# A planner's clock that counts each TensorE product at another length

## The chip, the cores and the metric

One Trainium2 chip, one core. The metric is the device time of one execution in microseconds (us), as the median of several runs.

## The reference

One inference step of a two-layer hybrid decoder, for 512 prompt tokens and 8 x 8 sample tokens (576 columns together). Cut to its core:

```python
for l in range(DEPTH):                      # 2 layers, D_MODEL 1024, D_FF 2816
    h = rmsnorm(x, norm_mix[l])
    proj = h @ w_in[l]                      # q, k, v, z, gates, pool and short-conv inputs
    o_a = delta_mixer(...)                  # conv, l2norm, chunked gated delta rule, 4 heads
    o_b = pool_mixer(...)                   # means over windows of 2, 4, 8, 16
    o_c = sc_b * causal_dwconv(sc_c * sc_x, ...)
    x = x + concat([o_a, o_b, o_c]) @ w_out[l]
    h = rmsnorm(x, norm_ffn[l])
    gate = causal_dwconv(h @ w_ffn_gate[l], ...)
    x = x + (silu(gate) * (h @ w_ffn_up[l])) @ w_ffn_down[l]
y = rmsnorm(x, final_norm)
```

## The kernel before

Tokens lie along the free axis: 576 columns in two halves of 288 (`HALVES`). Each f32 operand of a large product is split into a high and a low part of 32-bit "fp32r" type, and one weight tile times one half is three TensorE matmuls of 128x128 by 128x288 (`mm3`, lines 494 to 500). A weight piece holds four 128x128 tiles. It is loaded into `wraw`, its high part `whi` is copied by ScalarE (ACT) and its low part `wlo` is subtracted by VectorE (DVE) (`_split`, lines 145 to 153). One output tile `m` takes two pieces, 48 matmuls. Where the text counts products, it means these matmuls.

Each engine runs its instructions in the order in which the Python program writes them. That order is made by a planner at build time. `_Trunk.clock` holds one clock for each engine; `spend` (line 279) moves one of them by an operation's estimated cost. DVE, ACT and GpSimd (POOL) operations cost a fixed part and a part by the element (lines 207 and 208: 0.068 + n/960 us, 0.093 + n/1200 us and 0.1 + n/300 us, and 0.07 us more for a scale operand); a hand-over from one engine to another costs `hop`, 0.18 us. A TensorE product is counted in `mm` (line 457). "Now" is the planner's TensorE clock.

Small work (the triangular solves `tri`, `delta`, `sample`, the norms, the convolution tails) is written as generators, called streams. After each three products, `tick` (line 345) lets streams take a step if the end of their last step, plus a wait by name (`WAIT`), is not later than now. A stream of priority 1 is held back while the planner's DVE or ACT clock is more than 2.5 us ahead of now (`busy`, line 350). `room(2)` (line 390) at the start of each output tile forces stream steps, earliest first, until at most two PSUM banks wait to be read. `pump` (line 184) writes out the split of weight pieces up to two ahead of the piece that is in use.

The stretch that the prediction speaks of is the start of the feed-forward part in each layer. Its gate and up products are written in tiles m = 0, 1, 2, ... (even: gate of hidden group j = m/2; odd: up). Tiles 0 to 5 read the input before it is normalised, `fh` and `fl`, and scale their results; tile 6 is the first to read the normalised `nh` and `nl`. `normed` (lines 1785 to 1793) makes these in eight streams of an ACT copy, a POOL product, an ACT copy and a DVE subtraction, added when tile 2 starts (line 1999). `evac_gu` copies a gate tile into `gpad` with three DVE operations; `gate_tail` (line 1838) then makes two POOL copies, an ACT product and two DVE steps (`gcv`), an ACT tanh, and for j < 3 a DVE step (`gcv<-gth,gcv`) and two DVE products (`gth`); `up_tail` (line 1877) follows with two DVE products (`gp`), which empty the banks that `room` counts, and then splits the result (`hh`, `hl`).

Of the kernel before, what the change touches and what calls it, by code (L numbers as in the profile page):

```python
# [8 lines left out]
F32 = mybir.dt.float32  # L9
F32R = mybir.dt.float32r  # L10
F16 = mybir.dt.float16
# [229 lines left out]
class _Trunk:  # L241
# [209 lines left out]
    def mm(self, out, lhsT, rhs, start=True, stop=True):  # L451
        n = 1
        for d in rhs.shape[1:]:
            n *= d
        m = lhsT.shape[-1]
        f = lhsT.dtype
        self.spend("tensor", max(n * (4 if f == F32 else 1) / 2400.0, m / (4800.0 if f == F16 else 600.0 if f == F32 else 1200.0)) + 0.0025)
        self.nc.raw.tensor.matmul(out, lhsT, rhs, start=start, stop=stop)  # L458

    def rsqrt(self, v, n, name, eng):  # L460
# [1686 lines left out]
```

## Time and profile before

| | us |
|---|---|
| median of 3 runs (1520.3 to 1522.63) | 1522.19 |
| the profiled execution's own time | 1521.63 |
| its span, first to last instruction | 1519.9 |
| TensorE busy in the span | 1481.7 |
| DVE, ACT, POOL busy in the span | 1061.9, 681.5, 344.8 |

The span is the profiled execution's time without 1.7 us around it. "Busy" of TensorE (PE) counts overlapped matmuls, whose ends are modelled; so spacings of products are taken from starts or from rows that merge many. PEclk is the granted TensorE clock as a share of full speed: 1.00 is 2.4 GHz and 0.5 is 1.2 GHz.

### The profile page before, as it was taken

What the parts mean: (1) busy time and instruction counts of PE and PEld (TensorE: products, weight loads), DVE (VectorE), ACT (ScalarE), POOL (GpSimd) and SP (SyncE); (2) the same over time, 40 slices, a digit from 0 to 9 for tenths busy, and PEclk for the clock granted to TensorE, in tenths of its full rate; (3) what the DMA queues carried; (4) which work ended last, traced back from release to release, by engine and by line L of the source; (5) the groups of instructions that cost most, each with busy time, mean ns of one, the idle gap of its engine ahead of it and who ended that gap; (6) DMA issues with size and microseconds to landing.
All of it is one profiled execution on the core that took longest, in us unless ns stands there. A gap on an engine that the chain in (4) does not pass through costs nothing.

```text
span 1519.9 us, 29654 instructions
## 1 busy us (share of the span) xinstructions
PE 1481.7 (97%) x11438; PEld 1434.4 (94%) x11438; DVE 1061.9 (70%) x2253; ACT 681.5 (45%) x1453; POOL 344.8 (23%) x754
## 2 busy tenths in 40 slices
PE   9999999999899999999999999999989999999997
PEld 7999898899899999999999988989989999999997
DVE  7887776667973686377667987766588647854865
ACT  6445665545441344134533546754445324432442
POOL 2211022305511231122011111232083013301310
PEclk9999999999999999999999999999999999999998
DMA  5111122332223132222422112025212322232222
GB/s 199 61 56 43 47 74 85 129 99 70 84 83 99 63 105 84 84 97 73 142 76 67 57 45 91 22 85 171 77 57 91 97 71 97 77 93 96 77 82 84
DMA packets 67278, 128.78 MB, mean 85 GB/s; under 512 B 7952, under 2 KB 13248, under 8 KB 67136
## 3 DMA queue, kind: packets, MB, share of 16 engines
q1 hardware_dynamic: 59808, 105.15, 22.0%
q0 software_dynamic: 6208, 20.56, 3.8%
q8 instruction: 89, 1.46, 0.4%
q10 hardware_dynamic: 1120, 1.18, 0.2%
q14 instruction: 53, 0.43, 0.1%
HBM read 116.36 MB, written 10.49 MB: 83 GB/s over the span
## 4 chain that ended last, share of the span: by engine, by line
PE 86%; DVE 6%; issue 5%; ACT 1%; POOL 1%; DMA 1%; SPq 0%; POOLq 0%; DVEq 0%; ACTq 0%
PE ps L458 73%; PE q L458 12%; PE ps L229 2%; DVE wlo L229 1%; DVE gcv L229 1%; DVE m L229 1%; DMA xr<-in_x_dram 1%; DVE nl L229 1%; ACT m L229 1%; DVE cv L229 0%; DVE sqacc L229 0%; POOL kr_t L229 0%; DVE gth L229 0%; DVE xl L229 0%; DVE gpad L229 0%
## 5 line engine op out<-in xcount | busy, mean ns | idle before, releaser
L229 DVE TENSOR_TENSOR wlo<-wraw,whi 128x512 fp32r<-128x512 f32 (+1 forms) x432 | 315.9, 746 | 81.6 <-ACT whi L229 80.3
L229 ACT ACTIVATE whi<-wraw 128x512 fp32r<-128x512 f32 (+1 forms) x432 | 257.3, 613 | 158.7 <-PE ps L458 148.4
L458 PE MATMUL ps<-xh,whi 128*128 128x288 f32 x768 | 244.4, 318 | 0.1
L458 PE MATMUL ps<-xl,whi 128*128 128x288 f32 x768 | 228.9, 298 | 0.3 <-DVE xl L229 0.3
L458 PE MATMUL ps<-xh,wlo 128*128 128x288 f32 x768 | 228.2, 297 | 0.4 <-DVE wlo L229 0.4
L458 PE MATMUL ps<-nh,wlo 128*128 128x288 f32 x704 | 209.6, 298 | 13.3 <-DVE wlo L229 13.3
L458 PE MATMUL ps<-nh,whi 128*128 128x288 f32 x704 | 210.3, 299 | 0.0
L458 PE MATMUL ps<-nl,whi 128*128 128x288 f32 x704 | 209.7, 298 | 0.0
L458 PE MATMUL ps<-hh,whi 128*128 128x288 f32 x704 | 208.5, 296 | 0.0
L458 PE MATMUL ps<-hl,whi 128*128 128x288 f32 x704 | 207.6, 295 | 0.0
L458 PE MATMUL ps<-hh,wlo 128*128 128x288 f32 x704 | 207.0, 294 | 0.0
L458 PEld LDWEIGHTS ps<-xh,whi 128*128 128x128 f32 x768 | 146.1, 190 | 10.5 <-issue 7.9
L458 PEld LDWEIGHTS ps<-nh,wlo 128*128 128x128 f32 x704 | 134.7, 191 | 13.8 <-DVE wlo L229 13.8
L458 PEld LDWEIGHTS ps<-xh,wlo 128*128 128x128 f32 x768 | 146.4, 191 | 0.9 <-DVE wlo L229 0.9
L458 PEld LDWEIGHTS ps<-xl,whi 128*128 128x128 f32 x768 | 146.5, 191 | 0.8 <-DVE xl L229 0.7
L229 DVE SCALAR_TENSOR_TENSOR xr<-ps,xr 128x288 f32<-128x288 f32 x96 | 41.4, 457 | 140.4 <-PE ps L458 139.9
L458 PEld LDWEIGHTS ps<-nl,whi 128*128 128x128 f32 x704 | 134.1, 191 | 0.0
L458 PEld LDWEIGHTS ps<-nh,whi 128*128 128x128 f32 x704 | 134.1, 190 | 0.0
L458 PEld LDWEIGHTS ps<-hh,wlo 128*128 128x128 f32 x704 | 132.6, 188 | 0.0
L458 PEld LDWEIGHTS ps<-hl,whi 128*128 128x128 f32 x704 | 132.1, 188 | 0.0
L458 PEld LDWEIGHTS ps<-hh,whi 128*128 128x128 f32 x704 | 131.9, 187 | 0.0
L229 POOL TENSOR_TENSOR wraw<-wraw,wraw 128x512 f32<-128x512 f32 x48 | 74.9, 1559 | 109.1 <-DVE wlo L229 84.5
(313 smaller groups left out, 3335.3 us busy)
## 6 DMA issues: line engine op xcount, KB each, us to landing
wraw<-in_w_gu_dram SPq DMA_DIRECT2D x176, 256.0 KB, 2.9
wraw<-in_w_in_dram SPq DMA_DIRECT2D x96, 256.0 KB, 2.7
wraw<-in_w_dn_dram SPq DMA_DIRECT2D x80, 256.0 KB, 2.7
wraw<-in_w_out_dram SPq DMA_DIRECT2D x32, 256.0 KB, 2.8
xr<-in_x_dram POOLq DMA_DIRECT2D x12, 288.0 KB, 5.6
vs<-in_st_delta_dram POOLq DMA_DIRECT2D x6, 512.0 KB, 4.7
out_s_delta_dram<-vs POOLq DMA_DIRECT2D x6, 512.0 KB, 3.3
spill<-xr POOLq DMA_DIRECT2D x8, 288.0 KB, 2.4
```

What stands on the lines that cost most here:

```text
L229: return f(*args, **kw)
L458: self.nc.raw.tensor.matmul(out, lhsT, rhs, start=start, stop=stop)
```

## The change

`mm` counts a product differently; the instructions that it issues are the same. For the type of the large products the count was max(n/2400, m/1200) + 0.0025 us, with n columns and m weight columns; it becomes max(0.00044 n + 0.0025, 0.111 m/128) + 0.004. For f32 it was max(4n/2400, m/600) + 0.0025 and becomes max(0.00175 n + 0.0025, 0.224 m/128); for f16 it was max(n/2400, m/4800) + 0.0025 and becomes max(0.00042 n + 0.0025, 0.028 m/128).

```diff
         m = lhsT.shape[-1]
         f = lhsT.dtype
-        self.spend("tensor", max(n * (4 if f == F32 else 1) / 2400.0, m / (4800.0 if f == F16 else 600.0 if f == F32 else 1200.0)) + 0.0025)
+        per, least = {F32: (0.00175, 0.224), F16: (0.00042, 0.028)}.get(f, (0.00044, 0.111))
+        self.spend("tensor", max(n * per + 0.0025, least * m / 128.0) + (0.004 if f not in (F32, F16) else 0.0))
         self.nc.raw.tensor.matmul(out, lhsT, rhs, start=start, stop=stop)
```

## Rows read from the trace of the kernel before

**Rows 1.** The page: its span.

```profile
span 1519.9 us, 29654 instructions
```

**Rows 2.** Waits of PE, whole run: us in total, times, longest us.

```profile
PE ps L458 <- DVE wlo L229: 13.7, 4, 6.7
PE ps L458 <- DVE m L229: 3.3, 9, 0.5
PE ps L458 <- ACT m L229: 2.7, 2, 1.7
```

**Rows 3.** Windows of 40 us: length, busy us (instructions) by engine, PEclk, DMA share, GB/s.

```profile
160.00:200.00 40.00, 37.14 (x344) 34.07 (x344) 28.74 (x64) 24.80 (x64) 5.91 (x17) 0.96 0.25 84
...
400.00:440.00 40.00, 40.00 (x303) 40.00 (x302) 31.06 (x50) 19.52 (x38) 9.53 (x17) 1.00 0.31 94
```

**Rows 4.** Chain of work, feed-forward part: start us, us, what, count.

```profile
427.43 11.12 PE q L458 x84
438.56 64.00 PE ps L458 x480
```

**Rows 5.** Timeline of PE, mixer of layer 0: start us, us, instruction, count.

```profile
121.11 0.62 PE L458 MATMUL ps<-m 128*128 128x128 f16 x8
121.60 0.61 PE L458 MATMUL ps<-m,m 128*128 128x128 f16 x8
```

**Rows 6.** Timeline of PE where tile 6 starts: idle before it, and releaser, in brackets.

```profile
379.69 0.29 PE L458 MATMUL ps<-nl,whi 128*128 128x288 f32 x1
386.63 0.61 PE L458 MATMUL ps<-nh,wlo 128*128 128x288 f32 x1 [6.65 <-DVE wlo L229]
```

**Rows 7.** Windows around it, same columns as rows 3.

```profile
346.00:360.00 14.00, 14.00 (x108) 14.00 (x107) 3.20 (x8) 10.88 (x19) 6.92 (x7) 1.00 0.25 77
360.00:379.60 19.60, 19.60 (x149) 19.60 (x149) 19.34 (x25) 7.97 (x12) 13.87 (x15) 1.00 0.17 55
379.60:386.60 7.00, 0.38 (x3) 0.15 (x2) 6.93 (x10) 1.33 (x3) 6.69 (x7) 0.90 0.00 0
386.60:393.40 6.80, 6.77 (x32) 6.77 (x33) 6.73 (x8) 3.09 (x6) 6.41 (x7) 0.60 0.26 77
393.40:401.70 8.30, 8.30 (x65) 8.30 (x64) 8.30 (x13) 5.52 (x13) 3.69 (x8) 1.00 0.35 115
```

**Rows 8.** Timeline of ACT: the ACT product of gate group 0.

```profile
355.10 0.78 ACT L229 ACTIVATE gcv<-gpad,prm 128x592 f32<-128x592 f32 x1
```

**Rows 9.** Timeline of DVE in the same stretch.

```profile
356.42 0.84 DVE L229 TENSOR_TENSOR wlo<-wraw,whi 128x512 fp32r<-128x512 f32 x1 [2.67 <-ACT whi L229]
360.15 0.92 DVE L229 TENSOR_TENSOR gpad<-ps,rn 128x288 f32<-128x288 f32 x3 [2.89 <-PE ps L458]
360.99 4.59 DVE L229 TENSOR_TENSOR wlo<-wraw,whi 128x512 fp32r<-128x512 f32 x3
365.50 2.87 DVE L229 SCALAR_TENSOR_TENSOR gcv<-gpad,prm,gcv 128x592 f32<-128x592 f32 x2
...
375.05 1.69 DVE L229 SCALAR_TENSOR_TENSOR gcv<-gpad,prm,gcv 128x592 f32<-128x592 f32 x2
376.65 1.38 DVE L229 SCALAR_TENSOR_TENSOR gcv<-gth,gcv 128x592 f32<-128x592 f32 x1
378.07 1.94 DVE L229 TENSOR_TENSOR gth<-gcv,rn 128x512 f32<-128x512 f32 x2
379.93 2.10 DVE L229 SCALAR_TENSOR_TENSOR gcv<-gpad,prm,gcv 128x592 f32<-128x592 f32 x2
381.95 1.36 DVE L229 SCALAR_TENSOR_TENSOR gcv<-gth,gcv 128x592 f32<-128x592 f32 x1
383.35 1.89 DVE L229 TENSOR_TENSOR gth<-gcv,rn 128x512 f32<-128x512 f32 x2
385.16 0.81 DVE L229 TENSOR_TENSOR gp<-ps,gth 128x288 f32<-128x288 f32 x2
385.89 1.89 DVE L229 TENSOR_TENSOR wlo<-wraw,whi 128x512 fp32r<-128x512 f32 x2
```

## The prediction

> **What bounds the kernel now.** I read the page first, for the span [rows 1], then the waits of PE, the windows of 40 us, and the timelines of the one stretch that the waits point to. In the feed-forward part PE never pauses: its windows are full, at full clock [rows 3], and the chain there is products alone [rows 4]. No reordering can shorten that. What can move is what PE loses elsewhere, and one wait stands out: four waits on `wlo` make 13.7 us, the longest 6.7 [rows 2]. It comes where tile 6 starts, 6.65 us of idle [rows 6]. Layer 1 has its twin, since 13.7 is twice 6.65 and little more. The clock falls behind it: over the next 6.8 us PE is granted 0.60 and starts 32 products [rows 7], where at full clock it would start 6.8 / 0.1333 = 51. That is 6.8 - 32 x 0.1333 = 2.5 us more. So each layer loses 6.65 + 2.5 = 9.15 us there. DVE makes PE wait: from 360.0 to 386.6 it is busy 19.34 + 6.93 = 26.3 of 26.6 us, while in the 14 us before it is busy 3.2 [rows 7]. The second place is the mixer, with short waits on the `tri` chains' tiles (`m`): 3.3 us on DVE and 2.7 us on ACT over both layers [rows 2], and granted clocks of 0.96 in such a window [rows 3].
>
> **What the change counts.** For 288 columns the old line gives 288/2400 + 0.0025 = 0.1225 us, the new one 0.00044 x 288 + 0.0025 + 0.004 = 0.1332. The chain shows 11.12/84 = 0.1324 and 64.00/480 = 0.1333 [rows 4]. So now moves 8.7% more for each product, and is right. f16 products of 128 columns stay at 0.056 (0.0558 and 0.0563); eight of them take 0.49 us to the next eight [rows 5], 0.061 each. f32 products of 128 columns go from 0.216 to 0.227. The large products carry the effect. No instruction is added, removed or changed in cost, so the direct cost is nothing; what changes is the order on each queue.
>
> The Trainium skill has a rule that speaks against this: TensorE: Matmul & The Clock Gate, section "Wait — 56ns, not 53.3ns?", states N/2.4 GHz plus about 2.5 ns between starts at full clock, which at 288 columns is 122.5 ns, the old line exactly. By it the new line would count too long. The trace does not agree, with 132 to 133 ns here.
>
> **The start of the feed-forward part, step by step.** I follow the planner's clocks by its own lines. The eight `normed` streams start when tile 2 starts. Their ACT copies cost 0.093 + 576/1200 + 0.07 = 0.643 us each, 5.14 together, and the ACT product of gate group 0 behind them 0.656; with a hop of 0.18 it ends 5.98 us after tile 2 began. Tile 2 has 48 products: 5.88 us by the old count, 6.39 by the new one. So now the two DVE steps `gcv` of group 0 just miss the end of tile 2, by 0.10 us; after the change they make it, by 0.41 us. At the end of tile 2 stands the copy of gate tile 2, whose planned start lies behind eight POOL products of 0.1 + 576/300 = 2.02 us. It throws the planner's DVE clock some 12 us ahead, and with that every priority-1 stream is held back until the planner's wait for the next weights.
>
> The trace shows the result. ACT has finished group 0's product at 355.9 [rows 8], DVE idles 2.89 us up to 360.15, and the two steps run at 365.50, behind the copy and three `wlo`, for 2.87 us [rows 9]. In the new order they stand ahead of the copy and fill that idle time: 2.87 us less (1.69 where the same two steps run quicker) in the run of DVE that PE waits for.
>
> The second effect is at the start of tile 5, where `room(2)` forces group 0's two `gp`. Now group 0 is so late that the steps of groups 1 and 2 come earlier in the forced order: 2.10 us of `gcv`, 1.36 and 1.89 us of a later step and `gth` [rows 9] go ahead of the `wlo` that tile 6 needs. With group 0 finished before, only its `gp` is forced; these 2.10 + 1.36 + 1.89 = 5.35 us go behind that `wlo`. Together it is ready 2.87 + 5.35 = 8.2 us sooner: 386.6 - 8.2 = 378.4, or about 379.5 if some of the moved work runs at its slower durations, against PE's arrival at 379.7. The wait of 6.65 us goes, and with it the 2.5 us of clock.
>
> What is late next: the 5.35 us now stand before the `wlo` of tile 7's first piece, with one `wlo`, two `gp` and a split of `hh`, about 1 + 0.8 + 1.4 more. DVE is done with that at some 379.7 + 9 = 388.7; PE wants it 48 products after 379.7, at 386.1. A wait of 2.6 us, perhaps one of about 1 us for tile 8, and a shorter fall of the clock, some 1 us. So each layer gains 9.15 - 2.6 - 1 - 1 = 4.5; I take 5, since the later waits overlap. Bounds: 1.4 us, if only the time that DVE idles is won and in its quick form (1.69 less some 0.3 of the wait for the ACT part), and 9.15 if no new wait comes. Two layers: 10 us, between 3 and 18.
>
> **The mixer.** Steps of the small chains are written sooner in products: a step of 1.5 us is followed after 11.3 products, not 12.2. Forced bursts get shorter, since more was done before them, and cover of 0.13 us for each step is lost. Most steps have no wait on PE [rows 2], so I take zero here, with -3 to +6 us: the gain is at most about half of the 6.0 us of waits on `m`, the loss as much again as these waits.
>
> **The sum.** The profiled execution: 1521.63 - 10 = 1511.6. The median of the runs lies 0.56 above it: 1512.
>
> **The rivals.**
>
> Only half of it: the stall moves on to tiles 7 to 9, since DVE's work is the same and it is busy through 401.7 [rows 7]. For: DVE has no idle time there. Against: it idled just before, and full windows follow with DVE at 31 of 40 [rows 3]. Each layer gains 1.4: 1519.4. Chance 0.12.
>
> All of it: DVE's work behind tile 6 is spread thinly enough. 1522.2 - 18.3 = 1504. Chance 0.13.
>
> It does not do what it says here: another gate (the 2.5 us rule, a lack of pads) keeps group 0 behind the copy. The margin of 0.41 us is small, but the chain of ACT copies is anchored at tile 2's start in either count. 1522. Chance 0.08.
>
> Slower: the old count's missing 8.7% was cover, since the planner's DVE and ACT costs are short too: it counts a `wlo` at 0.60 us, and the trace has 0.84 and 1.53 [rows 9]. With the true product length, chains of `tri` reach PE before their data. If the waits on `m` double, 6.0 us more, with the boundary unchanged: 1528. It decides when a quarter or more of the small steps now arrive less than 0.2 us after their data. Against: only 11 waits are on `m`. Chance 0.17. If the skill's rule above held here, this cover would not exist at all and this case would be the likeliest.
>
> **How the numbers follow.** My forecast, the two gcv moved and most of the stall gone, has 0.50: 1512, by its own bounds 1504 to 1519. 1502 to 1524 takes in all but the slower case. A measurement of this kernel tells about 0.2%, 3 us, from no change. Faster: 0.50 + 0.13 + half of 0.12 = 0.69; within: 0.06 + 0.08 = 0.14; slower 0.17.
>
> **What would show it.** The timeline of DVE after `gcv<-gpad` x2 ahead of the `gpad` copy near 360, and fewer `gcv` and `gth` between it and the `wlo` that tile 6 waits for; PE's waits on `wlo` under 4 us a layer; a granted clock above 0.60 in the 6.8 us after tile 6 starts; full feed-forward windows as before; waits on `m` about 6 us. I am wrong if `gcv` still stands behind the copy, if the wait reappears whole at tile 7, or if waits on `m` grow past 10 us.

## The result, and the profile after

The changed kernel takes 1556.2 us (median of 4 runs, 1554.0 to 1557.3) against 1521.2 for the kernel before on the same chip: ratio 1.0227, 95% interval 1.0211 to 1.0243. It is 35 us slower; the prediction said 9 to 10 faster. The profiled execution took 1553.98 us, with a span of 1552.2. `mm` has one line more, so line 458 of before is L459 here.

The page of the kernel after: its span, and TensorE's busy time.

```profile
span 1552.2 us, 29696 instructions
PE 1498.4 (97%) x11438; PEld 1443.6 (93%) x11438; DVE 1077.2 (69%) x2253; ACT 681.3 (44%) x1453; POOL 366.2 (24%) x754
```

The waits of PE in it, to be laid beside [rows 2]: total us, times, longest.

```profile
PE ps L459 <- DVE m L229: 16.1, 15, 2.9
PE ps L229 <- ACT ms L229: 7.3, 2, 3.7
PE ps L459 <- DVE wlo L229: 6.7, 9, 1.5
```

The wait on `wlo` that the prediction was about is down from 13.7 to 6.7 us, and its longest from 6.7 to 1.5. But the waits on `m` have grown from 3.3 to 16.1 us, and one on `ms` (a tile of the `sample` chain) has appeared, twice 3.7 us.

Where the time went is seen best by product number: the start of the n-th large product in the two traces, and the difference. After is behind by 1.5 us at product 144, 3.0 at 864, 20.7 at 1152 (the end of layer 0's input projection) and 19.9 at 1824, where tile 6 of the feed-forward part starts. There it gains 9.3 us in its first 30 products, and gives back 5.1 by product 2400: 15.7 behind. Layer 1 repeats it: 18.4 behind at its product 864, 37.4 at 1152, 32.6 at the end. So the feed-forward start gains 4.2 us a layer and each mixer loses about 20, of which 17.7 and 19.0 us lie in the last six tiles of the input projection. The windows of that stretch, the same columns as [rows 3], after:

```profile
200.00:240.00 40.00, 36.65 (x313) 33.13 (x312) 27.41 (x72) 25.48 (x86) 7.32 (x35) 0.96 0.06 18
240.00:280.00 40.00, 35.47 (x237) 30.35 (x235) 20.56 (x59) 17.80 (x59) 9.90 (x43) 0.87 0.21 73
280.00:320.00 40.00, 38.08 (x230) 32.88 (x229) 22.48 (x51) 17.77 (x41) 13.07 (x42) 0.91 0.43 151
```

and before:

```profile
200.00:240.00 40.00, 40.00 (x361) 36.73 (x361) 29.71 (x72) 28.25 (x88) 8.05 (x39) 1.00 0.08 24
240.00:280.00 40.00, 39.74 (x263) 33.10 (x263) 25.02 (x77) 21.68 (x75) 15.44 (x61) 0.96 0.23 81
280.00:320.00 40.00, 38.85 (x277) 36.89 (x277) 25.24 (x55) 18.55 (x40) 7.49 (x20) 1.00 0.53 176
```

PE was busy in 97% or more of each of these windows; now it is in 89 to 95%, and DVE and ACT do less in each window, not more: they are not overloaded. The clock goes with the waits (0.87 and 0.91 of full speed: stretches at 0.5, the 1.2 GHz level, that follow PE's idle times). In layer 0, from the first large product to product 1152, PE's idle time goes from 5.6 to 17.6 us, and half of the time at half clock, which is about what it costs while PE is busy, from 5.1 to 11.9. Together that is 18.8 of the 20.7 us.

### The profile page after: what moved, and what is told of

It is laid out like the page before. It is cut to its first block, busy times and chain, and to the rows that moved or that the text cites. A ratio compares the mean times of both kernels' runs of the same rounds, so it can differ in the third digit from the quotient of the medians.

```text
span 1552.2 us, 29696 instructions
## 1 busy us (share of the span) xinstructions
PE 1498.4 (97%) x11438; PEld 1443.6 (93%) x11438; DVE 1077.2 (69%) x2253; ACT 681.3 (44%) x1453; POOL 366.2 (24%) x754
## 3 DMA queue, kind: packets, MB, share of 16 engines
q1 hardware_dynamic: 59808, 105.15, 21.8%
## 4 chain that ended last, share of the span: by engine, by line
PE 75%; DVE 10%; issue 6%; POOL 4%; ACT 4%; DMA 1%; SPq 0%; POOLq 0%; DVEq 0%; ACTq 0%
PE ps L459 62%; PE q L459 11%; DVE m L229 2%; PE ps L229 2%; DVE wlo L229 2%; ACT m L229 2%; POOL hl L229 1%; POOL hh L229 1%; DMA xr<-in_x_dram 1%; DVE gcv L229 1%; DVE nl L229 1%; DVE cv L229 1%; ACT whi L229 0%; ACT vs L229 0%; DVE fl L229 0%
## 5 line engine op out<-in xcount | busy, mean ns | idle before, releaser
L229 DVE TENSOR_TENSOR wlo<-wraw,whi 128x512 fp32r<-128x512 f32 (+1 forms) x432 | 314.2, 742 | 77.8 <-ACT whi L229 76.7
L229 ACT ACTIVATE whi<-wraw 128x512 fp32r<-128x512 f32 (+1 forms) x432 | 257.8, 614 | 163.5 <-PE ps L459 146.3
L459 PE MATMUL ps<-xh,whi 128*128 128x288 f32 x768 | 248.0, 323 | 1.9 <-ACT m L229 1.4
L459 PE MATMUL ps<-xl,whi 128*128 128x288 f32 x768 | 230.6, 300 | 0.6 <-DVE xl L229 0.6
L459 PE MATMUL ps<-xh,wlo 128*128 128x288 f32 x768 | 230.0, 299 | 0.2 <-DVE wlo L229 0.2
L459 PE MATMUL ps<-nh,wlo 128*128 128x288 f32 x704 | 208.2, 296 | 6.5 <-DVE wlo L229 6.5
L459 PE MATMUL ps<-nh,whi 128*128 128x288 f32 x704 | 208.3, 296 | 1.0 <-ACT whi L229 1.0
L459 PE MATMUL ps<-hh,whi 128*128 128x288 f32 x704 | 208.6, 296 | 0.0
L459 PE MATMUL ps<-nl,whi 128*128 128x288 f32 x704 | 207.7, 295 | 0.0
L459 PE MATMUL ps<-hl,whi 128*128 128x288 f32 x704 | 207.6, 295 | 0.0
L459 PE MATMUL ps<-hh,wlo 128*128 128x288 f32 x704 | 207.0, 294 | 0.0
L459 PEld LDWEIGHTS ps<-xh,whi 128*128 128x128 f32 x768 | 147.6, 192 | 14.5 <-issue 9.6
L459 PEld LDWEIGHTS ps<-xl,whi 128*128 128x128 f32 x768 | 148.4, 193 | 1.0 <-DVE xl L229 1.0
L459 PEld LDWEIGHTS ps<-xh,wlo 128*128 128x128 f32 x768 | 148.1, 193 | 0.4 <-DVE wlo L229 0.4
L459 PEld LDWEIGHTS ps<-nh,wlo 128*128 128x128 f32 x704 | 132.5, 188 | 8.5 <-DVE wlo L229 8.4
L229 DVE SCALAR_TENSOR_TENSOR xr<-ps,xr 128x288 f32<-128x288 f32 x96 | 41.4, 457 | 140.0 <-PE ps L459 139.6
L459 PEld LDWEIGHTS ps<-nh,whi 128*128 128x128 f32 x704 | 131.9, 187 | 1.5 <-ACT whi L229 1.5
L459 PEld LDWEIGHTS ps<-hh,wlo 128*128 128x128 f32 x704 | 132.6, 188 | 0.0
L459 PEld LDWEIGHTS ps<-hl,whi 128*128 128x128 f32 x704 | 132.1, 188 | 0.0
L459 PEld LDWEIGHTS ps<-nl,whi 128*128 128x128 f32 x704 | 132.1, 188 | 0.0
L459 PEld LDWEIGHTS ps<-hh,whi 128*128 128x128 f32 x704 | 131.9, 187 | 0.0
L229 POOL TENSOR_TENSOR wraw<-wraw,wraw 128x512 f32<-128x512 f32 x48 | 74.6, 1554 | 105.6 <-DVE wlo L229 80.4
```

Of the source, the lines that this page charges most:

```text
L229: return f(*args, **kw)
```

## The experiments

The first theory is that of the prediction's slower rival, called "lost cover": the count that was too short wrote each step of the mixer's chains later than its data, and the true count takes this margin away. The rival is "any other order": the change loses nothing of a margin that matters, it only lets the planner's choices fall otherwise, and other orders are worse than this one.

| run | count of a large product in the mixers, us | time, us | to its before, us |
|---|---|---|---|
| the change | 0.1332 | 1556.2 | +35.0 |
| e1_ffn_only | 0.1225 (old) | 1513.4 | -8.3 |
| e2_mixer_only | 0.1332, feed-forward part old | 1567.7 | +46.1 |
| e3_large_only | 0.1332, small products old | 1542.4 | +20.8 |
| e4_small_only | 0.1225, small products new | 1540.6 | +19.0 |
| e5_shorter | 0.1118 | 1567.9 | +45.9 |
| e6_plus1ns | 0.1235 | 1546.2 | +24.2 |
| e7_new_slack | 0.1332, 0.15 us delay | 1551.5 | +29.5 |
| e8_old_slack | 0.1225, 0.15 us delay | 1550.3 | +28.3 |
| e9_plus02 | 0.1227 | 1514.7 | -6.9 |
| e10_1295 | 0.1295 | 1523.6 | +1.9 |
| e11_1300 | 0.1300 | 1535.0 | +13.3 |
| e14_1360 | 0.1360 | 1544.0 | +21.8 |

The intervals reach 1.4 to 4.3 us to either side. The loss in the mixers is what a run stands above 1513.4: 43 us for the change (35.0 + 8.3). For e2 and e4, whose feed-forward part keeps the old count for the large products, it is what they stand above before. From e5 on, the feed-forward part has the new count, so 1513.4 is the time to which they compare (but for e7 the small products count anew too, as in the change).

**The two parts of the program apart.** A flag chooses the count; it is set when a layer's mixer begins and when its feed-forward part begins (e1: new there, e2: the reverse).

```diff
+        self.measured = False
...
+            self.measured = False
             self.mixer(l, xn, groups)
...
             xn = box["f"]
+            self.measured = True
...
+        if self.measured:
             per, least = ...
```

> The new count holds only while the feed-forward part of each layer is written; the start, both mixers and both output projections keep the old one. In the traces the feed-forward start of the changed kernel gains 4.2 us a layer by product number and its mixers lose about 20 us a layer. If the two parts are independent: 1521.2 - 2 x 4.2 = 1512.8 us, and the mixer's instruction order is that of before. If the gain needs the mixer's new order (its streams finish some 70 products earlier there), no gain: 1521.

> The reverse: the new count in the start, the mixers and the output projections, the old one in the feed-forward part. If the parts are independent: 1556.2 + 2 x 4.2 = 1564.6 us, with the wait on wlo at tile 6 back. If the mixer's loss is in truth paid back or made in the feed-forward part: under 1560.

Measured: 1513.4 and 1567.7. The parts are independent within the intervals: -8.3 and +46.1 add up to 37.8, where the whole change has 35.0. What the prediction worked out step by step is there, and all of the loss is the mixers'. As e1 keeps before's order in the mixers, it is also the best kernel of this study: 0.9943 of before, 0.9928 to 0.9958. The profiled execution of the change is 39.9 us longer than e1's; its PE is idle for 20.8 us more, and half of its time at half clock is 18.4 us more. So the mixers' loss is waiting, and the low clock around it, in nearly equal parts. Since layer 0 runs in it at the same time as in before, its windows can be laid on [rows 7]:

```profile
379.60:386.60 7.00, 6.87 (x52) 6.64 (x50) 6.93 (x9) 0.33 (x1) 6.77 (x7) 1.00 0.25 74
386.60:393.40 6.80, 5.43 (x41) 5.44 (x42) 6.76 (x9) 5.29 (x11) 6.49 (x6) 1.00 0.25 80
393.40:401.70 8.30, 7.32 (x56) 7.08 (x55) 8.30 (x9) 1.38 (x2) 7.91 (x9) 1.00 0.35 95
```

In the 7 us where PE started 3 products it now starts 52, and the clock stays at 1.00.

**Which count does it.** e3 has the new line for the large products alone, e4 for the f32 and f16 ones alone.

```diff
-        per, least = ...
-        self.spend(...)
+        if f not in (F32, F16):     # e4: if f in (F32, F16)
+            per, least = ...
+            self.spend(...)
+        else:
+            self.spend("tensor", max(n * (4 if f == F32 else 1) / 2400.0, ...) + 0.0025)
```

> New count for the large products alone, old count for the f32 and f16 products. Theory 'lost cover' (a product counted 8.7% longer lets the steps of the mixer's chains follow closer behind their data): nearly all of the loss stays, 1548 to 1560. Rival 'small products' (the f32 products counted 4 to 5% longer move the clock inside the stretches of small work, and that is what shifts the chains): the mixer's loss goes, 1510 to 1520.

> New count for the f32 and f16 products alone, old count for the large ones. Theory 'lost cover': as before within 5 us, 1517 to 1526, since a large product counts as before. Rival 'small products': 1545 or more. A second rival, 'any other order' (the named waits fit one order only, and any shift of it costs as much, whichever way it goes): 1530 to 1550.

Measured: 1542.4 and 1540.6. e3 lies between the ranges of both theories and fits neither. It has the feed-forward gain, so its mixers lose 29 us. In e4 a large product counts as before and yet 19 us are lost. That speaks for the second rival: an order need only be another one.

**Cover given and taken.** Three ways to write each step of the mixers later (e5: a shorter count; e7 and e8: a planned delay), and one count that takes a tenth of the new one's cover away (e6).

```diff
-            self.spend("tensor", max(...) + 0.0025)
+            self.spend("tensor", max(...) + 0.0025 + (0.0 if f in (F32, F16) else -0.0107))   # e6: 0.001
```
```diff
+            self.slack = 0.15        # e7 on the change, e8 on e1
             self.mixer(l, xn, groups)
...
             xn = box["f"]
+            self.slack = 0.0
```

> New count in the feed-forward part as in e1_ffn_only (1513.4 us); in the mixers a large product counts 0.1118 us, 8.7% of a product less than the old 0.1225, so each step of the chains is written later in products: more cover. Theory 'lost cover': the waits on m shrink, 1508 to 1518. Rival 'any other order' (the waits by name fit the one order for which they stand; any shift costs): 1525 to 1550, though every step has more cover.

> As e1_ffn_only (1513.4 us), but a large product in the mixers counts 0.1235 us, 1 ns more than the old count; the new one adds 10.7 ns. Theory 'lost cover': the loss goes with the count, at most a tenth of the 44 us that e2_mixer_only lost, 1514 to 1518. Rival 'any other order': the order changes at once and the time jumps, 1523 or more.

> The changed kernel (1556.2 us) with a planned delay of 0.15 us (slack) ahead of every step in the mixers; a step of 1.5 us lost 0.13 us of cover to the new count. Theory 'lost cover': most of the mixers' 44 us comes back, 1513 to 1528. Rival 'any other order': another order, and none of it that fits, 1535 to 1565.

> As e1_ffn_only (1513.4 us), old count in the mixers, with the same planned delay of 0.15 us ahead of every step there. Theory 'lost cover': more cover than before, 1508 to 1518. Rival 'any other order': 1525 to 1550.

Measured: 1567.9, 1546.2, 1551.5 and 1550.3. e5 lies above even the range of the second rival. e5 and e8 are 54.5 and 37 us slower than e1, and one nanosecond costs 33 us, more than all the 10.7 ns of e3 with its 29. e7, a third order, gets 5 us back where most of the 43 was expected.

How much cover a run has can be read from its hand-overs. In both mixers some 257 groups of small TensorE products (transposes aside) begin on data that DVE or ACT made for them. The program tells which instruction wrote it last, the trace when that one ended; the lead is the time from there to the first product. Before has a median of 1.27 us and 34 leads under 0.2 us.

| run | median lead, us | leads under 0.2 us | time, us |
|---|---|---|---|
| e1_ffn_only | 1.26 | 36 | 1513.4 |
| e6_plus1ns | 1.19 | 36 | 1546.2 |
| e8_old_slack | 1.35 | 35 | 1550.3 |
| e5_shorter | 1.50 | 39 | 1567.9 |
| the change | 0.93 | 50 | 1556.2 |
| e7_new_slack | 0.86 | 46 | 1551.5 |

With the cover of e1 (e6) or more (e5 and e8), and hardly more short leads, these three are 33 to 54.5 us slower. So a loss of this size needs no lost cover: another order is enough. The change did lose cover, though, and the delay in e7 did not bring it back, so e7 is no test of it. How much of the change's own 43 us is lost cover stays open.

**How much of the order must move.** By the planner's own order, 0.2 ns more (e9) moves 31 of the 1748 small TensorE instructions, each by three products; 1 ns moves 1036, by up to 66. e10, e11 and e14 are larger counts, the edit is that of e6 with 0.0002, 0.007, 0.0075 and 0.0135. They test whether the planner knows a bad order: its own TensorE clock stands still ahead of a small step whose data it expects later, for 42 us in both mixers with the old count, 37.5 in e10, 50.1 in e11, 41.2 in e14.

> As e1_ffn_only (1513.4 us), with 0.2 ns more for each large product in the mixers. In the planner's order that moves 31 of the 1748 small TensorE instructions, by three products each; 1 ns more (e6_plus1ns, 1546.2 us) moves 1036, by up to 66 products. Theory 'the order decides': 1511 to 1517. Rival 'the count decides, whatever it moves': 1518 or more.

> As e1_ffn_only, with 0.1295 us for a large product in the mixers, two thirds of the way to the new count. Here the planner's own TensorE clock stands still ahead of small steps for 37.5 us in both mixers, less than with the old count (42.3) and much less than half a nanosecond further (50.1, e11_1300). Theory 'a planned standstill is a real one': 1508 to 1520. Rival 'the waits by name fit the order of 0.1225 alone': 1530 to 1555. Theory 'lost cover': two thirds of the 44 us, 1540 to 1545.

> As e10_1295 with 0.1300 us; the planner's clock stands still for 50.1 us there. Theory 'a planned standstill is a real one': 10 to 25 us above e10_1295. Rival 'the waits by name fit one order alone': 1530 to 1555, within 8 us of e10_1295 or on either side. Theory 'lost cover': within 2 us of e10_1295.

> As e1_ffn_only, with 0.1360 us for a large product in the mixers, more than the new count's 0.1332; the planner's own TensorE clock stands still for 41.2 us ahead of small steps, as with the old count (42.0). Theory 'a planned standstill is a real one': 1513 to 1525. Theory 'lost cover': 13.5 / 10.7 of the 29 us that e3_large_only lost in the mixers, 1550. Rival 'any order but that of before': 1530 to 1555.

Measured: 1514.7, 1523.6, 1535.0 and 1544.0. e9 confirms that the order decides. e10 against e11 is half a nanosecond, 11.4 us on the chip and 12.6 in the planned standstill, though 1535.0 lies in the rival's range too. And e10 itself lies above the range of that theory, and e14 refutes that theory as a rule: planned like the old count, 31 us slower than e1. So the planner's standstill doesn't price an order. In e14 data has a median lead of 0.78 us only, so at long counts some lost cover may be part of the loss; over all counts the time isn't monotone (1513 at 0.1225, 1546 at 0.1235, 1524 at 0.1295, 1544 at 0.1360).

**One place of the loss.** In the kernel after, the chain of work shows what stands ahead of the 3.67 us wait on `ms` (start us, us, what):

```profile
250.19 0.19 POOL os_y L229
...
250.98 0.11 POOL vs L1456
251.09 0.52 issue
251.61 0.27 POOL cx L229 x2
251.88 0.02 issue
251.90 0.80 ACT sc L229
252.70 0.02 issue
252.72 0.85 DVE sc L229
253.57 0.02 issue
253.60 0.85 DVE sc L229
254.44 0.02 issue
254.47 0.82 DVE sc L229 x2
255.29 0.27 DVE ms L229
255.56 0.02 issue
255.58 0.66 ACT ms L229 x2
256.25 0.04 issue
256.29 0.37 PE ps L229
```

POOL is in a chain of small operations for a norm and then issues a DMA; the planner counts each such operation at 0.10 us and the trace has 0.28 from one to the next (`os_t` at 247.34, 247.61, 247.89). So the padding of the short convolution (`cx`) comes late, ACT's `sc` behind it, and DVE's queue stands still with four `sc` steps at its head. Behind them stands `ms`, for which PE waits. POOL's and ACT's part in this is read from the chain and was not tested; what was tested is the DVE steps. The timelines of ACT, DVE and PE, with the idle times:

```profile
251.90 0.79 ACT L229 ACTIVATE sc<-cx,prm 128x592 f32<-128x592 f32 x1 [4.22 <-POOL cx L229]
252.72 1.71 DVE L229 SCALAR_TENSOR_TENSOR sc<-cx,prm,sc 128x592 f32<-128x592 f32 x2 [1.52 <-ACT sc L229]
256.29 0.37 PE L229 MATMUL ps<-consts,ms 64*128 64x64 f32 x1 [3.67 <-ACT ms L229]
```

e12 leaves DVE's four steps of that convolution out (its output is then not computed); every queue's order is else that of the change, as the planner still counts them. e13 does the same in e1.

```diff
+            if skip:                      # first short convolution of a layer
+                self.spend("vector", 0.138 + n / 960)
+                continue
             nc.vector.scalar_tensor_tensor(out=out[:, 0:n], in0=t[:, i:i + n], ...
...
+                    else:
+                        self.spend("vector", 0.068 + 512 / 960)
+                        self.spend("vector", 0.068 + 64 / 960)
```

> The changed kernel (1556.2 us) in the same order on every queue, but the DVE steps of the first short convolution of each layer are left out (two products by taps and two by the norm; the planner still counts them), so that part of its output is not computed. In the changed kernel they wait on ACT's sc, ACT on POOL's cx, and the sample chain's ms stands behind them on DVE while PE waits 3.67 us. Theory 'head of line': that wait falls under 1 us and the half clock after it goes, 5 to 6.5 us a layer: 1543 to 1547. Rival 'PE waits there for the sample chain itself': 1552 to 1556.

> As e1_ffn_only (1513.4 us, mixers in the order of before), with the same DVE steps of the first short convolution left out as in e12_no_sc (that part of the output is not computed). Theory 'place': in this order DVE is idle only 0.1 us ahead of these steps and no sample step stands right behind them while PE waits, so they cost nothing: 1511 to 1515. Rival 'work': DVE's work itself is what PE waits for, so leaving out 3 us a layer gives most of the 14.6 us of e12_no_sc: 1499 to 1506.

Measured: 1541.6, which is 14.6 us less than the change and a little below the forecast, and 1513.3, no less than e1 (the runs spread by 2 to 6 us). PE's wait at the place in e12:

```profile
257.69 0.27 PE L229 MATMUL ps<-consts,ms 64*128 64x64 f32 x1 [0.66 <-ACT ms L229]
```

and the clock, in the window that starts where the wait ended in the kernel after; that kernel's line, and then e12's:

```profile
256.20:262.40 6.20, 6.11 (x20) 4.46 (x21) 1.49 (x4) 1.41 (x5) 0.00 (x0) 0.51 0.16 45
```
```profile
256.20:262.40 6.20, 5.54 (x36) 4.41 (x36) 2.18 (x5) 3.55 (x11) 0.37 (x4) 1.00 0.38 123
```

The wait is 3.0 us shorter, and the stretch at half clock is gone: PE starts 36 instructions in these 6.2 us, though the wait of 0.66 lies in them, against 20. As the order is the same, the two traces can be laid on each other start by start: e12 gains 5.6 us at this place in each layer (3.0 of the wait, 2.6 of the clock), and 1.6 more behind it. Its profiled execution was 4.4 us late before it came there in layer 0, part of it by stretches at half clock near 198 and 229 us that the change's trace has not. So where the clock falls differs from one execution to the next, and the two profiled ones are only 8.2 us apart. In the order of before the same steps cost nothing: DVE's idle time ahead of its eight `sc` tap products is 0.1 us in e1 and 3.2 us in the change (e1's line first). So it is not DVE's work but its place in the queue.

```profile
L229 DVE SCALAR_TENSOR_TENSOR sc<-cx,prm,sc 128x592 f32<-128x592 f32 x8 | 6.6, 829 | 0.1
L229 DVE SCALAR_TENSOR_TENSOR sc<-cx,prm,sc 128x592 f32<-128x592 f32 x8 | 6.7, 833 | 3.2 <-ACT sc L229 3.0
```

This one place is about a third of the mixers' 43 us. The rest, such as 2.85 us up to 210.8 us on `m` behind a `wlo` that waits for ACT, was read in the trace and not tried one by one.

## Why the prediction was wrong

**The counts.** Right. The chain after has 64.00 us for 480 products again, 0.1333 us each:

```profile
454.25 64.00 PE ps L459 x480
```

The rule of the Trainium skill that was weighed there (TensorE: Matmul & The Clock Gate, section "Wait — 56ns, not 53.3ns?") would give 122.5 ns for 288 columns, an estimate worked out from it; this trace too disagrees with it for these products, with 133.3. The slower case didn't hang on it.

**The start of the feed-forward part.** Right, nearly to the instruction. DVE's timeline after has the two `gcv` ahead of the three steps on `gpad`, in the time that was idle in [rows 9]:

```profile
376.33 0.85 DVE L229 TENSOR_TENSOR wlo<-wraw,whi 128x512 fp32r<-128x512 f32 x1 [2.68 <-ACT whi L229]
377.10 3.92 DVE L229 SCALAR_TENSOR_TENSOR gcv<-gpad,prm,gcv 128x592 f32<-128x592 f32 x2
380.94 0.87 DVE L229 TENSOR_TENSOR gpad<-ps,rn 128x288 f32<-128x288 f32 x3
381.74 2.96 DVE L229 TENSOR_TENSOR wlo<-wraw,whi 128x512 fp32r<-128x512 f32 x2
```

Tile 6 starts without a wait: 9.3 us gained, where 9.15 were counted. Then come the waits that were foretold for tiles 7 and 8, at 1.49 and 0.98 us where the sum had 2.6 and 1, and three smaller ones, 0.49, 0.20 and 0.57. The clock doesn't fall, against the 1 us foretold. Altogether 5.1 us are given back by product 2400, and 4.2 us a layer stay, where the sum had 4.5, rounded up to 5. That it comes so near is in part luck: the wait of tile 7 and the clock were priced too high, by 2.1 us, while the three smaller waits, and 1.4 us that is no idle time of PE, were in no term. e1 measures it alone: 8.3 us, for 10.

**The mixer.** This is the step that failed: "Most steps have no wait on PE [rows 2], so I take zero here, with -3 to +6 us". It was +43. The 6.0 us of waits on `m` in before (8.0 with two that L229's products have, which [rows 2] leave out) tell how good that one order is, not how the time answers to a change of order. The prediction saw that steps shift by a product or so and priced them as if each stayed between its neighbours. But a tick chooses by comparing clocks, and a step that falls one tick earlier changes what DVE has ahead of the next: 1 ns of count moves 1036 of 1748 instructions. The right price for this term was that of an unknown order: 10 to 54.5 us in the runs above that moved many steps. At the one place that was tried it was 3.0 us of waiting and 2.6 by the clock, in each layer.

**The slower rival.** It had the sign, and waits on `m` went above 10 us as it said. Its other mark, a quarter of the steps with a lead under 0.2 us, was not reached by the count above: 19%, up from 13%. Its price of 6 us was a seventh of the loss, since it too scaled the waits of before. Cover was lost, but orders with as much cover as before, or more, are as slow, so its mechanism is not needed for the loss, and its share is not known. What was shown at the place that was tried is late small work at the head of a queue, with the clock falling behind the wait.

**The range.** 1502 to 1524 held only cases that keep the mixer's order. All the bounds came from rows of one order.

## What to carry to other kernels

Where a planner at build time sets the order, correcting one of its constants isn't a small change, however right the constant: it draws another order, and here the waits of the old profile said nothing about the new one. Bring such a correction in only where its effect was followed step by step (here the feed-forward part, 8.3 us faster), and keep the order elsewhere. When PE waits, go up the queue of the engine that it waits for to the first instruction with idle time ahead of it, and try that one before you blame the engine's load.

## What was not expected of the hardware

Small dependent operations on POOL, one to four elements to a partition, start 0.28 us after one another, and a DMA issue there took another 0.63 us; in the chain above, the padding of a convolution that stood behind them came late, and PE waited behind ACT and DVE. A wait of PE of 3.7 us was followed by 6.2 us at a granted clock of 0.51, and when the wait was 0.66 us the clock stayed at 1.00; start by start that was worth 2.6 us on top of the wait. In the feed-forward start five waits of 0.2 to 1.5 us left the clock at 1.00. The length of the last wait alone doesn't tell, though: in the change's mixer one of 0.78 us at 284.0 us stands just before 6.8 us at half clock.
